# Hybrid attention and PEER layer on one core: gather steps moved between the attention heads and the query stage

## The chip, the cores and the metric

One Trainium2 chip, one of its cores. The metric is the device time of one execution of the program, in microseconds (us). Engines are called as in the profile: PE (TensorE matmuls) and PEld (its weight loads), DVE (VectorE), ACT (ScalarE), POOL (GpSimd), SP (SyncE, here only a DMA queue).

## The reference, cut to what matters

One decoder layer over 512 tokens of 1024 values. First a mixer: 8 heads of dilated window attention (head group A), 8 heads of stick-breaking attention (head group B), one output projection, a layer norm. Then PEER: each token picks 128 of 16384 single-neuron experts and takes a gated sum over them; a second layer norm.

```
mix = hybrid_mixer(x, w_in[layer], w_out[layer])
x = layer_norm(DEEPNORM_ALPHA * x + mix, ...)
...
q = (x @ w_query).reshape(b, s_len, PEER_HEADS, 2, PEER_KEY_DIM // 2)
scores = einsum('bshpc,hpnc->bshpn', q, sub_keys)      # 8 heads x 2 halves x 128 keys
top_s, top_i = lax.top_k(scores, PEER_TOPK)            # 16 of each half
...
best_s, best_pos = lax.top_k(cand_s, PEER_TOPK)        # 16 of the 256 sums
gates = jax.nn.softmax(best_s, axis=-1)
...
u = jnp.take(expert_u, ib, axis=0)
h = jnp.einsum('td,ted->te', xb, u)
act = gb * jax.nn.gelu(h, approximate=False)
vv = jnp.take(expert_v, ib, axis=0)
y = jnp.einsum('te,ted->td', act, vv)
```

## The kernel before

The 512 tokens are four blocks of 128. The PEER sum is done in two ways. For blocks 0 and 1 the kernel **gathers**: for each of the 128 chosen experts of a token, one indirect DMA from the POOL queue brings one row of `peer_u` (later of `peer_v`) per token, 128 rows of 4 KB, 512 KB in all. For blocks 2 and 3 it computes all 16384 experts **densely** on PE: `h` products with streamed `uT` tiles (L849), Gelu, a product with a scattered gate table, and `y` products with streamed `peer_v` tiles (L1106).

There are 512 gathers, numbered in order: 0 to 127 are `peer_u` for block 0, 128 to 255 `peer_v` for block 0, then the same for block 1. `gather(n)` (L732) issues one. `gather_use(n)` consumes one on DVE: a `peer_u` gather is one multiply-and-sum (L741), a `peer_v` gather one multiply-and-add (L752; the second one is a plain scaling, L749). After gather 127 the 128 sums go through Gelu on ACT (L743), DVE scales `x` (L744), and before gather 128 DVE multiplies the sums by the gates (L747), which waits for that Gelu. The generator `gathers` uses one gather per step and keeps eight further ones issued (nine buffers), up to `limit`, which is 256 until block 1 is routed. `take(n)` takes n such steps. 64 gathers are used before the part of the program that the change touches.

That part is written out by hand (`tc.manual_schedule()`): each engine runs its instructions in the order in which the loops emit them.

- **The heads** (loop over i from -1 to 33). 32 tasks: eight heads of group A for block 3 and eight of group B for block 1 mixed (tasks 0 to 15), then eight of group B for block 2 (16 to 23) and for block 3 (24 to 31). A task is a generator of six steps spread over four iterations. For group B (`head_b`): scores on PE (L341, L343), three activations (L347 to L349), one DVE operation (L351, emitted in iteration i = its task number), cumulative sums on PE (L353, L355, one iteration later), an exponential (L357), the product with the values on PE (L361). Each iteration ends with some gather steps.
- **The fills**. From i = 16 on the output projection of block 1, from i = 28 on that of block 2 is filled in, two steps per iteration (`next(fill, None)`): `project_out` has four steps of two products (L499) for each half c, then `add_out` on DVE (L459 and its half statistics, L145); then `normalize` in three steps: statistics with two tiny activations (L160, L161) and L514 on DVE; L163 to L166 and L519 on DVE; transposes on PE (L172) with copies by ACT (L525). `epilogue` copies and transposes a finished head group (L372, L172, L396).
- **Behind the loop**: the last epilogue (block 3) with gather steps between, what is left of the fill, `project_out(3)` with a gather step after each of its steps, and `normalize(3)` with two gather steps.
- **The query stage** (loop over it from 0 to 17): PE computes a query projection (`q_mm`, L597, L599) and scores (`q_scores`, L610, copied by ACT at L612); two iterations later DVE finds the best 16 of each row for three blocks, in five rounds of three operations (`topk_ops`, L536 to L544), with a gather step after each of the first QGATH rounds. `run_ahead` puts in pieces of the dense `h` products.
- **Behind it**: `route_steps(2)` on DVE, then 64 steps that build the gate table while `route_steps(3)` and `route_steps(1)` run, then the dense stage, in which all gathers that are left are spread evenly (`pre` is the count used so far).

Of the kernel before, what the change touches and what calls it, by code (L numbers as in the profile page):

```python
# [74 lines left out]
KT = 6  # L75
MIXB = (5, 4, 2)
PRE0 = 64
QGATH = 4
QH = 2
PRE1 = 7  # L80
GSTEP = 24
# [11 lines left out]
def build(ctx, nc, tc, a):  # L93
# [45 lines left out]
    def bank(nm):  # L139
        if nm == "mm":  # L140
            nm = next(mm_banks)
        return (ps_h if nm == "h" else ps_f).tile([P, 512], F32, name=nm, bufs=2 if nm == "h" else 1)
# [161 lines left out]
    def group(tb):  # L304
        st = {"po": bank("h")}
        for n_ in ("nm", "z", "rz"):
            st[n_] = work.tile([P, NH], F32, name=n_, bufs=3)
        return st
# [80 lines left out]
    def xcol(tb, ks):  # L389
        return x1[:, ks] if tb == 1 else xf[:, ks, (tb - 2) * P:(tb - 1) * P]  # L390
# [10 lines left out]
    def epilogue(kind, tb, st):  # L401
        o = (close_a if kind == "a" else close_b)(st)
        yield
        place([(o, tb, 0 if kind == "a" else 4)])
        yield
# [22 lines left out]
    def chain(*steps):  # L428
        for s_ in steps:
            yield from s_  # L430
# [17 lines left out]
    def head(steps, n):  # L448
        for _ in range(n):
            if next(steps, steps) is steps:  # L450
                return
            yield
# [4 lines left out]
    def add_out(tb, c, ps):  # L457
        sl = slice(c * 512, (c + 1) * 512)
        nc.vector.scalar_tensor_tensor(x2[:, tb, sl], x2[:, tb, sl], ALPHA, ps, op0=OP.mult, op1=OP.add)  # L459
        if c == 0:  # L460
            sts[tb] = stats_tile()
        half_stats(x2[:, tb], sts[tb], c)
# [30 lines left out]
    def project_out(tb):  # L493
        for c in range(2):
            ps = bank(("m2", "tr")[c])
            for kq in range(4):
                for k in range(2):
                    kk = 2 * kq + k
                    nc.tensor.matmul(ps, xcol(tb, kk), wo[c, kq][:, k], start=kk == 0, stop=kk == KD - 1)  # L499
                yield  # L500
            add_out(tb, c, ps)

    def normalize(tb):
        t = [] if tb == 0 else ln1
        if tb == 0:
            for n in ("ln1_g", "ln1_b"):
                t.append(wst.tile([P, D], F32, name="w", bufs=WBUF))
                nc.sync.dma_start(t[-1], a[n].to_broadcast([P, D]))
        r = x2[:, tb]
        s_ = stats_steps(sts[tb])  # L510
        mv = next(s_)
        halves = [slice(g * 512, (g + 1) * 512) for g in range(2)]
        for sl in halves:
            nc.vector.scalar_tensor_tensor(r[:, sl], r[:, sl], mv[:, 0:1], t[0][:, sl], op0=OP.subtract, op1=OP.mult)  # L514
        if tb:
            yield
        mv, rs = next(s_)
        for sl in halves:
            nc.vector.scalar_tensor_tensor(r[:, sl], r[:, sl], rs, t[1][:, sl], op0=OP.mult, op1=OP.add)  # L519
        yield  # L520
        for g in range(2):
            tr = transpose4(r[:, g * 512:(g + 1) * 512], "a" if g and tb == 0 else "tr")
            ks = slice(4 * g, 4 * g + 4)
            if tb:
                nc.scalar.activation(xcol(tb, ks), tr, AF.Copy)  # L525
            else:
                nc.scalar.activation(x0(ks), tr, AF.Copy)
        yield
# [396 lines left out]
    with tc.manual_schedule():  # L925
        def take(n):
            for _ in head(gs, n):
                pass
# [8 lines left out]
        for i in range(-1, NTASK + 2):  # L937
            def go(j):
                if 0 <= j < NTASK:
                    next(live[j])  # L940

            next(lo_, None)
            new = i + 1 < NTASK
            if new:
                kind, tb, h = tasks[i + 1]
                if h == 0:
                    sts_[kind, tb] = group(tb)
                live[i + 1] = (head_a if kind == "a" else head_b)(tb, h, sts_[kind, tb], ("a", "b", "m0", "m1")[(i + 1) % 4])
                go(i + 1)
            go(i)  # L950
            for g_ in list(after):
                if next(g_, g_) is g_:
                    after.remove(g_)
            if new:
                go(i + 1)
            next(fill, None)
            go(i - 1)
            go(i - 1)
            take(2 if i >= 14 else i % 4 > 0)
            next(fill, None)  # L960
            if i >= 2:
                go(i - 2)
                kind, tb, h = tasks[i - 2]
                if h == NH - 1:
                    after.append(epilogue(kind, tb, sts_[kind, tb]))
            if (fill_at := {16: 1, 28: 2}.get(i)):
                fill = chain(fill, project_out(fill_at), normalize(fill_at))
        for g_ in after:
            for _ in g_:
                take(1)  # L970
        for _ in fill:
            pass
        qs.close()
# [6 lines left out]
        for _ in project_out(3):  # L980
            take(1)
# [9 lines left out]
        for it in range(18):  # L991
# [7 lines left out]
            if it >= 2:  # L999
                ops = [topk_ops(tb, it - 2, scs[it - 2][:, t]) for t, tb in enumerate(PARTS[1])]  # L1000
                for r in range(5):
                    for o_ in ops:
                        next(o_)
                    if r < QGATH:
                        take(1)
# [232 lines left out]
```

## Time and profile before

| what | us |
|---|---|
| median of 3 runs | 1536.68 |
| the 3 runs | 1536.68, 1538.01, 1508.45 |
| the profiled execution, its own time | 1511.87 |
| its span, first to last instruction | 1510.1 |

Over the span PE is busy for 92%, DVE 80%, POOL 45%, ACT 34%. The page's 40 slices of 37.8 us show three stretches: up to slice 21 the DMA rate swings between 163 and 393 GB/s; in slices 22 to 37 it stands at 406 to 410 GB/s; the last three slices are the end of the dense stage and the final norms. The granted PE clock is 0.96 over the whole. "Busy" of PE is modelled, so the reader looks for the engine whose instructions follow each other without a gap and whom others wait for, stretch by stretch.

### The profile page before, as it was taken

The page shows a single profiled execution, that of the slowest core. Times are in us where ns is not written, and L with a number is a line of the kernel's source. Part 1 is how long each engine was busy: PE and PEld are TensorE (multiplying, and loading weights), DVE is VectorE, ACT ScalarE, POOL GpSimd, SP SyncE. Part 2 cuts the span into 40 slices and gives each one's busy share as a digit, 9 for nine tenths or more (in the row PEclk, how much of TensorE's full clock was granted, in tenths as well). Part 3 has the DMA queues.
Part 4 walks back from the last instruction along what each step waited for, and adds up shares of the span by engine and source line. Part 5 has one row for each costly group of instructions (what it writes and reads, how often), then busy time and mean ns, then how long its engine had stood idle before and what let it go on. Part 6 is the DMA issues. An engine that isn't in the chain of part 4 may idle for free.

```text
span 1510.1 us, 19683 instructions
## 1 busy us (share of the span) xinstructions
PE 1382.3 (92%) x6686; PEld 1120.0 (74%) x6686; DVE 1203.2 (80%) x2481; ACT 507.0 (34%) x1059; POOL 682.2 (45%) x526
## 2 busy tenths in 40 slices
PE   7989888999989998288889999999999999999796
PEld 3658676776659987277678888888888888878575
DVE  0128988886669999999998877778778878788887
ACT  1422333453412111199952222222223222222342
POOL 0000476754555444302556555555556556566200
PEclk9889999999999999599999999999999999999898
DMA  8756799896689999568999999999999999999872
GB/s 287 232 172 229 281 336 330 294 393 209 206 302 331 367 312 363 163 220 268 288 329 410 410 408 410 410 409 409 409 410 410 409 410 410 410 409 406 334 247 93
DMA packets 163220, 495.94 MB, mean 328 GB/s; under 512 B 15376, under 2 KB 48288, under 8 KB 163120
## 3 DMA queue, kind: packets, MB, share of 16 engines
q0 software_dynamic: 74304, 270.13, 47.6%
q1 hardware_dynamic: 86432, 218.66, 39.6%
q10 hardware_dynamic: 2384, 5.90, 1.0%
q8 instruction: 53, 0.87, 0.2%
q14 instruction: 47, 0.39, 0.1%
HBM read 477.78 MB, written 16.84 MB: 328 GB/s over the span
## 4 chain that ended last, share of the span: by engine, by line
DMA 36%; PE 27%; DVE 23%; issue 8%; ACT 4%; POOL 2%; SPq 0%; ACTq 0%; POOLq 0%; DVEq 0%
DMA g<-peer_u,eidx 17%; DMA g<-peer_v,eidx 14%; PE y L1106 5%; PE h L849 4%; DVE yg L752 4%; DVE x L752 3%; POOL g L732 2%; DMA v<-peer_v 2%; ACT o L815 2%; PE m L261 2%; PE m L499 1%; DVE o L806 1%; PE tr L499 1%; DVE vl L123 1%; DVE g L741 1%
## 5 line engine op out<-in xcount | busy, mean ns | idle before, releaser
L732 POOL DMA_INDIRECT g<-peer_u,eidx x256 | 343.2, 1341 | 388.8 <-DVE topi L544 145.7
L732 POOL DMA_INDIRECT g<-peer_v,eidx x256 | 333.1, 1301 | 338.0 <-DVE x L752 101.3
L849 PE MATMUL h<-xf,w 128*128 128x256 f32 x2048 | 475.4, 381 | 7.4 <-ACT gl L841 7.4
L849 PEld LDWEIGHTS h<-xf,w 128*128 128x128 f32 x2048 | 385.0, 191 | 60.3 <-ACT gl L841 7.8
L741 DVE SCALAR_TENSOR_TENSOR g<-g,x 128x1024 f32<-128x1024 f32 x256 | 307.7, 1222 | 71.0 <-DMA g<-peer_u,eidx 69.6
L1106 PE MATMUL y<-vh,a 128*128 128x512 f32 x928 | 289.6, 417 | 14.2 <-ACT a L1092 10.1
L1106 PEld LDWEIGHTS y<-vh,a 128*128 128x128 f32 x928 | 176.3, 191 | 56.6 <-ACT a L1092 13.0
L752 DVE SCALAR_TENSOR_TENSOR x<-g,hg,x 128x1024 f32<-128x1024 f32 x128 | 163.8, 1279 | 28.6 <-DMA g<-peer_v,eidx 27.3
L752 DVE SCALAR_TENSOR_TENSOR yg<-g,hg,yg 128x1024 f32<-128x1024 f32 x126 | 161.4, 1281 | 18.1 <-DMA g<-peer_v,eidx 16.4
L123 DVE TENSOR_TENSOR vl<-v,vh 128x1024 fp32r<-128x1024 f32 x122 | 148.8, 1220 | 23.1 <-ACT vh L1061 21.9
L1106 PE MATMUL y<-vl,a 128*128 128x512 f32 x464 | 147.5, 400 | 0.7 <-DVE vl L123 0.7
L1061 ACT ACTIVATE vh<-v 128x1024 fp32r<-128x1024 f32 x122 | 128.6, 1054 | 40.8 <-DMA v<-peer_v 22.0
L1092 ACT ACTIVATE a<-gl 128x512 fp32r<-128x512 f32 x58 | 36.5, 629 | 268.5 <-DVE gl L1086 233.9
L841 ACT ACTIVATE gl<-h 128x256 f32<-128x256 f32 x128 | 48.3, 378 | 222.9 <-PE h L849 213.0
L1106 PEld LDWEIGHTS y<-vl,a 128*128 128x128 f32 x464 | 87.8, 190 | 22.0 <-DVE vl L123 2.0
L815 ACT ACTIVATE o<-o1b,sg 128x128 f32<-128x128 bf16 x256 | 83.4, 400 | 2.7 <-DVE o1b L800 2.4
L261 PE MATMUL m<-w,x0f 128*128 128x256 f32 (+1 forms) x128 | 48.5, 520 | 9.1 <-DMA x0f<-xT 7.9
L821 PEld LDWEIGHTS m<-o,o 128*128 128x128 f32 x304 | 39.0, 195 | 21.1 <-ACT o L815 14.4
L821 PE MATMUL m<-o,o 128*128 128x128 f32 x304 | 42.9, 285 | 12.1 <-ACT o L815 5.6
L127 PE MATMUL m<-wl,x2h 128*128 128x512 f32 x96 | 41.1, 428 | 9.8 <-DVE wl L123 9.7
L806 DVE TENSOR_TENSOR o<-sg,c_small 128x512 f32<-128x512 f32 x64 | 43.8, 685 | 0.7 <-PE a L821 0.6
L261 PEld LDWEIGHTS m<-w,x0f 128*128 128x128 f32 x128 | 24.0, 200 | 26.6 <-issue 11.1
(261 smaller groups left out, 1859.5 us busy)
## 6 DMA issues: line engine op xcount, KB each, us to landing
w<-uT SPq DMA_DIRECT2D x128, 512.0 KB
v<-peer_v SPq DMA_DIRECT2D x128, 512.0 KB
w<-w_in SPq DMA_DIRECT2D x47, 512.0 KB
gt<-gd SPq DMA_DIRECT2D x15, 960.0 KB
w<-peer_wq SPq DMA_DIRECT2D x16, 512.0 KB
wq<-peer_wq SPq DMA_DIRECT2D x16, 512.0 KB
gd<-stage SPq DMA_DIRECT2D x15, 512.0 KB
gd<-stage SPq DMA_DIRECT2D x15, 448.0 KB
```

Source lines behind the costliest of these rows:

```text
L123: nc.vector.tensor_sub(parts[1], src, parts[0].bitcast(F32))
L261: nc.tensor.matmul(ps[:, ch * wd:(ch + 1) * wd], x0f[:, kk], w[:, k], start=kk == 0, stop=kk == KD - 1)
L732: nc.gpsimd.indirect_dma_start(out=u, out_offset=None, in_=a["peer_v" if kind else "peer_u"], in_offset=bass.IndirectOffsetOnAxis(ap=eidx[ ...
L741: nc.vector.scalar_tensor_tensor(u, u, 1.0, x, op0=OP.mult, op1=OP.mult, accum_out=hs[:, j:j + 1])
L752: nc.vector.scalar_tensor_tensor(acc, u, hs[:, j:j + 1], acc, op0=OP.mult, op1=OP.add)
L806: nc.vector.tensor_tensor(hot2[s], gate[tb][1][:, 0, t:t + TG, None].to_broadcast([P, TG, P]), iota[:, None, :].to_broadcast([P, TG, P]), ...
L815: nc.scalar.activation(hot[s][:, j], o1b[:, :, j], AF.Copy, scale=gate[tb][1][:, 1, t + j:t + j + 1])
L821: nc.tensor.matmul(gps[s][:, j * P:(j + 1) * P], o2[:, j], o1[:, j], start=True, stop=True)
L841: nc.scalar.activation(gls[c // 2][:, c % 2], ps[:, :ND], AF.Gelu)
L849: nc.tensor.matmul(hps[c][:, :ND], us[c][:, k], xf[:, k], start=k == 0, stop=k == KD - 1)
L1061: nc.scalar.activation(vsp[c][0], vs[c], AF.Copy)
L1106: nc.tensor.matmul(yps[t][hf], s_, w_[:, hf * 512:(hf + 1) * 512], start=c == 0 and n == 0, stop=c == P - 1 and n == len(terms) - 1)
```

## The change

Three counts and one extra step change; no instruction is new.

- `QGATH` goes from 4 to 3: three gather steps for each query iteration from it = 2 on instead of four.
- In the loop over the heads the iterations from i = 24 on take three gather steps instead of two.
- The last epilogue takes two gather steps after each of its two steps instead of one.
- `project_out` gets one more `yield` between the products of half 0 and its `add_out`. In a fill, the `add_out` of half 0 and all that follows come half an iteration later; in `project_out(3)` it is one more gather step.

```diff
-QGATH = 4
+QGATH = 3
...
                     nc.tensor.matmul(ps, xcol(tb, kk), wo[c, kq][:, k], start=kk == 0, stop=kk == KD - 1)
                 yield
+            if c == 0:
+                yield
             add_out(tb, c, ps)
...
             go(i - 1)
             go(i - 1)
-            take(2 if i >= 14 else i % 4 > 0)
+            take(3 if i >= 24 else 2 if i >= 14 else i % 4 > 0)
             next(fill, None)
...
         for g_ in after:
             for _ in g_:
-                take(1)
+                take(2)
```

## Rows read from the trace of the kernel before

**Rows 1.** Stages: length, busy us per engine (instructions), granted PE clock, DMA share, GB/s
```profile
371.60:425.70 54.10, 54.10 (x274) 37.95 (x272) 29.77 (x51) 22.59 (x37) 26.16 (x21) 0.99 0.65 213
...
425.70:449.50 23.80, 18.42 (x48) 8.95 (x48) 18.72 (x36) 2.68 (x6) 14.94 (x10) 0.86 0.87 330
...
465.80:598.40 132.60, 125.18 (x723) 113.85 (x722) 132.60 (x449) 18.29 (x41) 63.78 (x66) 0.97 0.95 345
...
598.40:640.50 42.10, 12.99 (x53) 10.67 (x52) 40.92 (x136) 5.73 (x13) 13.93 (x12) 0.64 0.57 191
...
640.50:775.00 134.50, 116.72 (x740) 98.42 (x739) 131.56 (x353) 123.55 (x354) 44.13 (x23) 0.99 0.82 263
...
775.00:1430.00 655.00, 640.12 (x2838) 538.13 (x2837) 534.10 (x687) 171.18 (x263) 371.83 (x277) 0.99 1.02 406
```

**Rows 2.** Timeline, query stage, DVE: start, length, instruction [idle before]
```profile
465.83 0.67 DVE L536 MAX8 top<-sc 128x8 f32<-128x128 f32 x3
...
590.70 1.28 DVE L752 SCALAR_TENSOR_TENSOR yg<-g,hg,yg 128x1024 f32<-128x1024 f32 x1
...
591.89 0.10 DVE L538 MATCH_VALUE_LOAD topi<-top,sc 128x8 f32 x1
...
598.41 0.42 DVE L1017 CAST iob<-c_small 128x512 bf16<-128x512 f32 x1
```

**Rows 3.** Timeline, query stage, PE
```profile
550.81 0.83 PE L610 MATMUL m<-skT,qT 128*128 128x128 f32 x6
...
557.58 0.83 PE L610 MATMUL m<-skT,qT 128*128 128x128 f32 x6
...
559.12 0.83 PE L610 MATMUL m<-skT,qT 128*128 128x128 f32 x6
```

**Rows 4.** Timeline behind the heads, PE and DVE
```profile
424.21 0.69 DVE L459 SCALAR_TENSOR_TENSOR x<-x,tr 128x512 f32<-128x512 f32 x1 [6.98 <-PE tr L499]
...
427.30 1.22 DVE L741 SCALAR_TENSOR_TENSOR g<-g,x 128x1024 f32<-128x1024 f32 x1
...
429.59 0.15 DVE L163 TENSOR_TENSOR lw<-lw 128x1 f32<-128x1 f32 x1
...
431.25 1.09 PE L172 MATMUL tr<-c_ident,x 128*128 128x128 f32 x4 [3.52 <-DVE x L519]
...
433.93 8.70 PE L499 MATMUL m<-wo,xf 128*128 128x512 f32 x16
...
442.47 7.03 PE L499 MATMUL tr<-wo,xf 128*128 128x512 f32 x16
```

**Rows 5.** Timeline around gather 127's Gelu, ACT and DVE
```profile
460.81 1.28 ACT L743 ACT_TABLE_LOAD   x1
...
462.10 0.31 ACT L743 ACTIVATE hg<-hg 128x128 f32<-128x128 f32 x1
...
462.45 0.29 DVE L747 TENSOR_TENSOR hg<-hg,gate 128x128 f32<-128x128 f32 x1 [3.48 <-ACT hg L743]
...
463.62 0.49 ACT L612 ACTIVATE sc<-m 128x384 f32<-128x384 f32 x1 [0.18 <-PE m L610]
```

**Rows 6.** Timeline, the first fill's norm, PE
```profile
362.19 0.78 PE L361 MATMUL h<-v,su 128*128 128x64 f32 x6
...
363.76 0.23 PE L343 MATMUL m<-maskb,identb 128*128 128x128 bf16 x1
...
366.35 1.12 PE L172 MATMUL tr<-c_ident,x 128*128 128x128 f32 x4 [2.36 <-DVE x L519]
...
371.62 1.17 PE L361 MATMUL h<-v,su 128*128 128x64 f32 x6
```

**Rows 7.** Timeline, head tasks 27 and 28, DVE and PE
```profile
386.63 0.69 DVE L351 SCALAR_TENSOR_TENSOR su<-m,su 128x512 f32<-128x512 f32 x1 [1.10 <-ACT su L349]
...
393.37 1.08 PE L353 MATMUL m<-su,c_tri 128*128 128x512 f32 x2
```

**Rows 8.** Chain of waits, dense stage: start, length, what
```profile
1049.46 20.30 DMA g<-peer_u,eidx
```

## The prediction

> **What bounds the kernel now.** I read the slices of the page first, then the busy times by stage, then the timeline of the stages that the change touches, and the waits there. The slices part the run at about 790 us: behind it the DMA rate is flat, ahead of it it is not. The stage rows [rows 1] say who sets the pace. Over the heads of block 3 (371.6 to 425.7 us) PE is busy for all of 54.10 us and DVE for 29.77: PE sets it, DVE has 24 us free. In the query stage (465.8 to 598.4) DVE is busy for all of 132.60 us. In the routing and the gate table (598.4 to 775) DVE has 40.92 of 42.10 and 131.56 of 134.50. From 775 to 1430 the DMA share is 1.02 at 406 GB/s. So ahead of 775 us the engines decide, and what they save up to there starts the dense stage earlier by as much; behind it bytes decide, and each gather not used by then is paid at the DMA rate.
>
> **Gather steps counted.** Before: 64 early, 51 in the loop over the heads (11 up to i = 13, two in each of the 20 iterations behind), 2 in the last epilogue, 8 in `project_out(3)`, 2 in its norm: 127 when the query stage begins; then 2 + 2 + 16 x 4: 195 at its end. After: 64 + 61 + 4 + 9 + 2 = 140, and 4 + 16 x 3 more: 192. So 16 steps leave the query stage, 13 go to the heads and the stretch behind them, 3 are left to the dense stage.
>
> **Query stage: -19.0 us.** DVE begins the first round at 465.83 and the routing's first operation at 598.41 [rows 2]: 132.6 us for 16 iterations, 8.29 each. A `peer_v` step costs from its start at 590.70 to the next instruction at 591.89, 1.19 us [rows 2] (less than the 1.28 shown, since ends overlap). 16 x 1.19 = 19.0; an iteration comes to 7.10. PE needs from 550.81 to 557.58, 6.77 us, for the same iteration [rows 3], and had put out its last scores at 559.12, 39 us ahead of DVE [rows 2, 3]. So DVE still sets the pace, but by 0.33 us per iteration only.
>
> **The extra half step in the first fill: -3.0 us (0 to -4.5).** Block 1's norm stops PE: behind its instruction at 363.76 it waits until 366.35 for L519 (2.36 us), and comes back slow [rows 6]. The product that took 0.78 at 362.19 takes 1.17 at 371.62 [rows 6], so the 6.4 us between 366.35 and the end of that one hold some 2.1 us lost. With the extra `yield`, L163 to L519 are emitted ahead of the gather steps of iteration 22 instead of behind those of iteration 21, and the transposes behind the cumulative sums of task 21 instead of ahead of them. PE has work in the wait. 2.36 + 2.1 = 4.5 at most; nothing if DVE's order leaves the wait as it is. I take 3, nearer to the most, since PE's work between is there.
>
> **The third step in iterations 24 to 33: 0 us.** A `peer_u` step costs half of 427.30 to 429.59, 1.145 us [rows 4]; ten more are 11.5 us in 24 us of DVE's free time [rows 1]. A step of the heads asks 0.69 [rows 7] + 3 x 1.145 = 4.1 us of DVE; PE takes 54.1/10 = 5.4 per iteration [rows 1], less for the first few. DVE falls back there by a microsecond or two, but task 27's L351 starts at 386.63 and PE reads it at 393.37 [rows 7]: six microseconds in hand. If that cover were gone, the ten steps would cost their 11.5. In transfers the stage had 213 GB/s; ten gathers of 0.524 MB in 54.1 us add 97: 310, against 406 in the dense stage [rows 1].
>
> **Behind the heads: +2.5 us (to +7.9).** Here the change costs. The chain is: L459 of half 1 at 424.21, statistics and L514, two gather steps from 427.30, L163 at 429.59, transposes on PE at 431.25, `project_out(3)` from 433.93 [rows 4]. Three things alter.
> First, in PE's order the value product of task 30 now stands ahead of half 1's last products: +1.0 by [rows 6] (six products 0.78, eight about 1.0).
> Second, four gather steps stand between L514 and L163, not two, and by the count above they are 125 to 128. So Gelu's wait falls in here: three steps (3.44), then ACT's Gelu and DVE's multiply and step 128. From Gelu's start at 462.10 to L747 at 462.45 is 0.35 [rows 5]; with 0.2 before it, 0.29 for L747 and 1.19 for the step I count 5.5 in place of 2.3, +3.2. PE, its transposes, and all of `project_out(3)` are queued behind L163. The table load of 1.28 [rows 5] runs while DVE is still in steps 125 to 127; without that cover it is 1.28 more.
> Third, this wait leaves the query stage, where DVE stood 3.48 us for Gelu [rows 5]. The first scores were copied by 464.11 [rows 5] and DVE came 1.7 later [rows 2]; now it finds them ready: -1.7.
> Sum 1.0 + 3.2 - 1.7 = 2.5. PE's pause grows by about 4 us, and behind the present one (granted clock 0.86 over this stage [rows 1]) half 0 takes 8.70 us against 7.03 for half 1 [rows 4]; were all of half 0 at the lower clock level, it would be 14.06: +5.4, the upper end. The ninth step in `project_out(3)` lies in DVE's wait for these products.
>
> **Three gathers later: +3.9 us (0 to 3.9).** 3 x 0.524 MB at 406 GB/s [rows 1]. Nothing, if PE and not DMA spaces the dense stage: PE is busy for 640 of its 655 us [rows 1]. I take the DMA's price, as its share is the full one.
> A page of the Trainium skill speaks of this rate: HBM Reference, Specifications, gives about 358 GB/s as a core's share with both cores of a memory domain streaming, and about 425 for a core alone. By the share the three would cost 4.4 (estimate), the sum would be half a microsecond worse. The stage here moves 406, nearer to the figure for a core alone.
>
> **Sum.** -19.0 - 3.0 + 0 + 2.5 + 3.9 = -15.6 us. Against the profiled execution's 1511.87 that gives 1496.3. That execution lies 24.8 below the median shown; the three runs lie at 1508.45 and at 1536.68 and 1538.01, 28 apart for one and the same program, more than this change moves. Set against the median, the sum gives 1521.1, my number; the range must hold both places. The sum's own bounds: -19.0 - 4.5 + 2.5 + 0 = -21 and -19.0 + 0 + 7.9 + 3.9 = -7.2.
>
> **Rivals.**
> *The gap behind the heads eats half* (0.20). The PE clock stays low over half 0 and the first fill gains nothing: -7.2, 1529.5. For it: PE's clock falls at each pause of this size in the trace [rows 4, 6]. Against: half of the lower rate is already in the 8.70.
> *PE spaces the dense stage* (0.10). Then the three gathers are free: -19.5, 1517.2. For it 640 of 655, against it a DMA share of 1.02 [rows 1].
> *Nothing is left* (0.09). What DVE saves is lost ahead of 775 us, by PE's pace in the query stage: its margin is 0.33 us per iteration, and 16 iterations longer by 1.0 for a late weight tile would take the 15.6. 1536.7. Against: PE ran its 16 iterations without such a wait while the DMA carried 345 GB/s [rows 1, 3], and fewer gathers ask for less.
> *Slower: gathers land too late* (0.06). With eight ahead, a landing of T gives a gather each T/8. In the dense stage one took 20.30 us [rows 8], 2.54 each: three would take 7.6 us where an iteration of the heads lasts 5.4 and one of the query stage 7.1. Ten times 2.2, and 16 times 0.5: +30, in sum +14: 1551. It begins to cost at 3T/8 = 5.4, a landing of 14.4 us. Against: four gathers per 8.29 us came without a gap in DVE's 132.60 [rows 1, 2], so they landed within 16.6 us, at a higher rate (345 GB/s) than the 310 asked of the heads.
> The forecast itself has 0.55.
>
> **Range and chances.** Its lower end is the lowest run less 21: 1487; its upper end is the highest run less 5, 1533, which takes in the forecast, PE-spaced and half-eaten cases wherever the runs fall. 2% of the median, about what a measurement of this kernel can tell from no change, is 31 us; no case of gain reaches it alone. Faster by over 2% takes runs that fall at the lower place more often than before: 0.13. Slower by over 2% takes late landings at their worst together with the higher place: 0.04. Within 2%: 0.83.
>
> **What would show it.** In the changed profile: query iterations of 7.1 us on DVE with no idle, and their whole stretch near 113.5; L519 of block 1's norm followed by transposes without a two-microsecond stop of PE; no wait of L351's readers in the heads; L743 between the last epilogue and `normalize(3)`, L163 some 5.5 us behind L514, `project_out(3)` about a microsecond later than before (-3 + 4.2); the DMA plateau starting some 19 us earlier. It is wrong if DVE waits for gathers or scores before 600 us, or if the plateau starts earlier and the end does not.

## The result and the profile after

| | us |
|---|---|
| before, median of 9 runs beside those of after | 1510.87 (1508.45 to 1543.34) |
| after, median of 9 runs | 1518.97 (1493.44 to 1526.99) |
| ratio after : before, executions of one kind | 0.9916, 95% interval 0.9889 to 0.9942 |

Executions of either kernel come in two lengths some 28 us apart (a stretch at half PE clock from 300 us on, called the early half clock below, makes the longer one), the medians mix them, and the ratio compares only the shorter ones. So the change takes off 0.84%: 12.7 us of 1510.87, between 8.8 and 16.8. The sum of the prediction, -15.6, lies inside that interval. The profiled execution of after has the early half clock, so it is read stage by stage. Its line numbers behind L500 are two higher than those of before (L741 is L743).

The page of after, its span and the granted PE clock in 40 slices of 38 us, in tenths:

```profile
span 1522.9 us, 19706 instructions
...
PEclk9889999957998999799999999999999999999898
```

The 5 and the 7 in the ninth and tenth slice are the half clock: 300 to 364 us, ahead of most of what the change touches. Stages of after, the columns as in [rows 1]: a window in the low clock; block 3's heads; the stretch to L459; the query stage; the routing; the dense stage:

```profile
350.00:360.00 10.00, 10.00 (x47) 9.32 (x46) 7.57 (x15) 4.72 (x10) 5.50 (x4) 0.50 0.50 157
371.60:425.70 54.10, 52.55 (x282) 38.12 (x281) 44.58 (x81) 29.21 (x52) 34.10 (x23) 1.00 0.63 204
425.70:450.30 24.60, 24.60 (x101) 15.02 (x101) 18.19 (x32) 4.34 (x7) 20.03 (x16) 1.00 0.91 318
495.60:609.00 113.40, 113.40 (x677) 104.08 (x676) 113.40 (x432) 18.62 (x39) 44.95 (x48) 1.00 0.92 319
609.00:651.00 42.00, 23.03 (x102) 19.63 (x101) 41.26 (x137) 7.19 (x17) 13.27 (x11) 0.80 0.65 221
794.00:1430.00 636.00, 623.19 (x2776) 524.81 (x2776) 516.32 (x666) 163.81 (x255) 378.15 (x271) 0.99 1.03 409
```

DVE's 44.58 us in the heads stand against 29.77 in [rows 1]: the third step. The query stage lasts 113.40 us against 132.60, and DVE is busy for all of it. The dense stage moves 409 GB/s against 406.

Where the time went, between marks that both kernels have (the start of an instruction each, in order: first L499 of the first fill, L351 of tasks 24 and 31, the first MAX8 of the query stage, the routing's cast, the first gate-table operation, the last `y` product). The third column sets after against another execution of before with the same early half clock (h2_before_again, below); the fourth sets a second profile of after without it (e1_all) against the profile of before.

| stretch | forecast | after, both with the early half clock | after, both without it |
|---|---|---|---|
| first fill up to task 24 | -3.0 | -5.0 | -3.8 |
| task 24 to task 31 | 0 | +1.5 | **+6.9** |
| task 31 to the first MAX8 | +2.5 | +3.0 | +3.3 |
| query stage | -19.0 | -19.0 | -19.1 |
| routing | 0 | -0.2 | 0.0 |
| gate table and dense stage | +3.9 | +5.1 | +4.8 |
| sum | -15.6 | -14.6 | -7.9 |

Five of six lines are near their terms. One is not: task 24 to 31 in the fourth column, 6.9 us, about half of the gain. That column belongs to one execution of 1501.37 us, the second longest of the six of e1_all (1492.38 to 1504.27): its stages sum to -7.9, where the ratio of all six (0.9913) makes -13.1. So not every execution need lose as much there. And ahead of the first fill, where no edit but the last below reaches, the eleven profiles without the early half clock differ by 12 us (first L499 at 325.7 to 338.1), so single executions are compared by stage and not by their time.

**The query stage**, timeline of DVE and of PE (start, length, instruction):

```profile
495.57 0.68 DVE L538 MAX8 top<-sc 128x8 f32<-128x128 f32 x3 [3.68 <-ACT sc L614]
...
524.53 1.26 DVE L754 SCALAR_TENSOR_TENSOR x<-g,hg,x 128x1024 f32<-128x1024 f32 x1
525.71 0.08 DVE L540 MATCH_VALUE_LOAD topi<-top,sc 128x8 f32 x1
...
609.04 0.40 DVE L1019 CAST iob<-c_small 128x512 bf16<-128x512 f32 x1
```

```profile
580.70 0.83 PE L612 MATMUL m<-skT,qT 128*128 128x128 f32 x6
...
587.47 0.83 PE L612 MATMUL m<-skT,qT 128*128 128x128 f32 x6
...
589.00 0.83 PE L612 MATMUL m<-skT,qT 128*128 128x128 f32 x6
```

As [rows 2, 3] with one step less: 113.47 us in 16 iterations, 7.09 each; a step still takes 1.18; PE still needs 6.77 and ends 20 us ahead of DVE instead of 39.

**Behind the heads**, DVE, then PE, then ACT:

```profile
450.33 0.69 DVE L459 SCALAR_TENSOR_TENSOR x<-x,tr 128x512 f32<-128x512 f32 x1 [0.77 <-PE tr L499]
...
453.42 1.22 DVE L743 SCALAR_TENSOR_TENSOR g<-g,x 128x1024 f32<-128x1024 f32 x1
...
457.58 0.28 DVE L749 TENSOR_TENSOR hg<-hg,gate 128x128 f32<-128x128 f32 x1
...
459.10 0.15 DVE L163 TENSOR_TENSOR lw<-lw 128x1 f32<-128x1 f32 x1
...
479.42 0.69 DVE L459 SCALAR_TENSOR_TENSOR x<-x,tr 128x512 f32<-128x512 f32 x1 [0.68 <-PE tr L499]
...
482.51 1.28 DVE L754 SCALAR_TENSOR_TENSOR x<-g,hg,x 128x1024 f32<-128x1024 f32 x1
483.70 0.15 DVE L163 TENSOR_TENSOR lw<-lw 128x1 f32<-128x1 f32 x1
```

```profile
460.76 1.09 PE L172 MATMUL tr<-c_ident,x 128*128 128x128 f32 x4 [6.92 <-DVE x L521]
...
463.45 9.07 PE L499 MATMUL m<-wo,xf 128*128 128x512 f32 x16
472.35 7.03 PE L499 MATMUL tr<-wo,xf 128*128 128x512 f32 x16
```

```profile
454.50 1.28 ACT L745 ACT_TABLE_LOAD   x1
456.97 0.31 ACT L745 ACTIVATE hg<-hg 128x128 f32<-128x128 f32 x1 [1.19 <-DVE g L743]
...
481.30 0.20 ACT L160 ACTIVATE lw<-lw 128x1 f32<-128x1 f32 x1 [15.72 <-DVE mv L157]
481.52 1.28 ACT L161 ACT_TABLE_LOAD   x1
482.82 0.20 ACT L161 ACTIVATE lw<-lw 128x1 f32<-128x1 f32 x1
```

L459 to L163 takes 8.77 us against 5.38 in [rows 4]; three steps, Gelu, the gates' product and step 128 stand between, and Gelu's table load (454.50) is hidden behind steps 125 to 127, as was said. PE's pause is 6.92 us against 3.52, and half 0 behind it 9.07 against 8.70. New is the load at 481.52: it stands between L160 and L161 of `normalize(3)`, which in before ran back to back (451.42 and 451.65). It costs nothing: L161 is done at 483.02, while DVE is in a gather step until 483.70, and L163 starts there. That is 4.28 us behind L459 (479.42), against 4.23 in before (449.54 and 453.77), where no load stood.

**The heads**, DVE and POOL:

```profile
413.45 0.69 DVE L351 SCALAR_TENSOR_TENSOR su<-m,su 128x512 f32<-128x512 f32 x1
...
417.48 0.69 DVE L351 SCALAR_TENSOR_TENSOR su<-a,su 128x512 f32<-128x512 f32 x1
...
437.72 1.23 DVE L743 SCALAR_TENSOR_TENSOR g<-g,x 128x1024 f32<-128x1024 f32 x1 [1.44 <-DMA g<-peer_u,eidx]
```

```profile
412.35 1.98 POOL L734 DMA_INDIRECT g<-peer_u,eidx  x1 [0.30 <-issue]
414.64 1.44 POOL L734 DMA_INDIRECT g<-peer_u,eidx  x1 [0.30 <-issue]
```

Iterations follow each other on DVE by 4.03 us, near the 4.1 worked out. PE waits nowhere for L351. But POOL issues one gather in 1.74 to 2.29 us (the instruction and 0.30 behind it), some 6.0 for three, and DVE uses three in 4.03. From 422 to 438 us DVE waits seven times for a gather, 0.2 to 1.4 us each, 5.6 in all. Its last step ends at 449.56, 0.8 ahead of PE's products for L459. The work still fits, and there is hardly any room left.

### The profile page after: what moved, and what is told of

Its sections match the earlier page's. It is cut to its first block, busy times and chain, and to the rows that moved or that the text cites. A ratio compares the mean times of both kernels' runs of the same rounds, so it can differ in the third digit from the quotient of the medians.

```text
span 1522.9 us, 19706 instructions
## 1 busy us (share of the span) xinstructions
PE 1410.8 (93%) x6686; PEld 1141.9 (75%) x6686; DVE 1202.9 (79%) x2481; ACT 511.4 (34%) x1062; POOL 697.2 (46%) x526
## 4 chain that ended last, share of the span: by engine, by line
PE 35%; DMA 31%; DVE 21%; issue 7%; ACT 4%; POOL 2%; another core or an unknown queue 0%; SPq 0%; ACTq 0%; POOLq 0%; DVEq 0%
DMA g<-peer_v,eidx 14%; DMA g<-peer_u,eidx 12%; PE y L1108 8%; PE h L851 8%; DVE x L754 3%; DVE yg L754 3%; DMA v<-peer_v 2%; POOL g L734 2%; ACT o L817 2%; PE m L499 2%; PE m L261 2%; DVE o L808 1%; PE tr L499 1%; PE h L333 1%; PE h L361 1%
## 5 line engine op out<-in xcount | busy, mean ns | idle before, releaser
L734 POOL DMA_INDIRECT g<-peer_u,eidx x256 | 353.0, 1379 | 385.0 <-DVE topi L546 145.2
L734 POOL DMA_INDIRECT g<-peer_v,eidx x256 | 338.3, 1322 | 340.8 <-DVE yg L754 94.7
L743 DVE SCALAR_TENSOR_TENSOR g<-g,x 128x1024 f32<-128x1024 f32 x256 | 306.5, 1222 | 60.5 <-DMA g<-peer_u,eidx 59.0
L261 PEld LDWEIGHTS m<-w,x0f 128*128 128x128 f32 x128 | 24.7, 205 | 25.7 <-issue 11.9
```

What stands on the lines that cost most here:

```text
L261: nc.tensor.matmul(ps[:, ch * wd:(ch + 1) * wd], x0f[:, kk], w[:, k], start=kk == 0, stop=kk == KD - 1)
L734: nc.gpsimd.indirect_dma_start(out=u, out_offset=None, in_=a["peer_v" if kind else "peer_u"], in_offset=bass.IndirectOffsetOnAxis(ap=eidx[ ...
L743: nc.vector.scalar_tensor_tensor(u, u, 1.0, x, op0=OP.mult, op1=OP.mult, accum_out=hs[:, j:j + 1])
```

## The experiments

Theory: the terms of the sum are right, and what the fourth column loses is PE's clock behind block 1's norm, where the fill now stands differently. Rivals: the third step in the heads takes it (by POOL's pace), or Gelu's new place does.

**The whole change again.** There is no edit against after.

> The whole change once more, for a second execution to read by stages. The theory of the sum (DVE sets the query stage, PE hides the third step in the heads, each gather left over is paid at the DMA rate in the dense stage): about 13 to 16 us shorter than before, query stage from its first MAX8 to the routing's first cast 113.5 us in place of 132.6, dense stage 3 to 4 us longer. The rival that descriptor generation on POOL, and not PE, sets the end of the heads: DVE's last gather steps of the heads lie behind the last output projection product of block 2, and the heads end several us later than before. A further suspicion from the profile after: the norm of block 3 shows a second activation table load of 1.28 us between its two tiny activations, 1.3 us on the way to the query stage; it should be there again.

Measured: 1495.3 us median, ratio 0.9913 (0.9879 to 0.9947), so the first result holds. Its stages stand in the table above. PE at the norm of the first fill, then PE's clock from 360 us on (columns as in [rows 1]):

```profile
362.54 0.66 PE L172 MATMUL tr<-c_ident,x 128*128 128x128 f32 x4 [0.88 <-DVE x L521]
363.89 0.66 PE L172 MATMUL tr<-c_ident,x 128*128 128x128 f32 x4 [0.69 <-ACT x L527]
...
365.26 2.07 PE L341 MATMUL a<-qB,kB 64*128 64x128 f32 x8
...
383.61 1.16 PE L341 MATMUL m<-qB,kB 64*128 64x128 f32 x8
```

```profile
360.00:365.00 5.00, 3.44 (x23) 2.61 (x21) 4.86 (x11) 3.02 (x6) 0.44 (x1) 0.98 0.02 3
365.00:370.00 5.00, 5.00 (x17) 3.87 (x17) 3.56 (x8) 2.12 (x4) 4.08 (x4) 0.50 0.47 128
370.00:375.00 5.00, 5.00 (x20) 4.05 (x19) 3.76 (x7) 1.77 (x4) 2.99 (x4) 0.50 0.86 320
375.00:380.00 5.00, 5.00 (x21) 4.40 (x20) 4.12 (x7) 1.44 (x3) 1.62 (x2) 0.50 0.83 285
380.00:385.00 5.00, 5.00 (x24) 3.37 (x23) 3.23 (x6) 2.90 (x6) 3.65 (x4) 0.81 0.64 197
```

The wait for the norm has shrunk from 2.36 us [rows 6] to 0.88, and the 0.69 for ACT's copy behind it is left, as in before. Then PE, busy without a gap, stands at half clock (1.2 GHz instead of 2.4) for more than 15 us: eight products take 2.07 us instead of 1.16. In before the windows of 5 us behind its longer wait show a shorter stretch:

```profile
365.00:370.00 5.00, 2.96 (x10) 2.26 (x11) 4.89 (x11) 1.88 (x4) 2.96 (x3) 0.56 0.62 175
370.00:375.00 5.00, 5.00 (x24) 4.01 (x24) 2.47 (x5) 1.39 (x3) 3.69 (x4) 0.76 0.72 219
375.00:380.00 5.00, 5.00 (x37) 4.43 (x36) 3.65 (x7) 3.75 (x7) 1.68 (x1) 1.00 0.68 238
```

**One part each.** First `QGATH` alone:

```diff
-QGATH = 4
+QGATH = 3
```

> Only the third step per query iteration: nothing is taken earlier, so 16 gathers are left to the dense stage. Theory of the sum: the query stage is 19.0 us shorter, the dense stage 16 x 1.29 = 20.6 us longer, in all +1.6 us, no difference to be measured. Rival, that the gain of the change is the shorter query stage itself and the dense stage has room for gathers (PE spaces it): about -15 to -19 us.

Measured: 1.0023 (1.0002 to 1.0044), some +3.5 us. The query stage is 113.44 us, 19.1 less; gate table and dense stage together are 21.0 longer than the mean of three profiles with before's count of gathers (862.9 us, see below), 1.31 per gather for 16 gathers. Taking steps out of the query stage is worth nothing by itself; the gain comes from where they go.

The extra `yield` alone:

```diff
+            if c == 0:
+                yield
```

> Only the extra yield ahead of the first add_out (and the one gather step more that it brings in the last output projection). Theory of the sum: 3.0 us less in the norm of block 1 (PE's stop of 2.4 us gone), 1.0 us more behind the heads, one gather fewer in the dense stage (-1.3), in all -3.3 us. Rival, that PE stops there as long as before because DVE's order leaves the wait: 0 to -1.3 us.

Measured: 0.9969 (0.9948 to 0.999), -4.7 us, near the -3.3 expected. Its profile (1509.19 us, the second longest of nine at 1501.33 to 1510.7) shows less: up to task 24's L351 it gains 3.9 us, from there to task 31 it loses 3.9 again (35.39 us against 31.53; granted clock 0.74 from 366 to 386 us), and its stages sum to -1.0. The heads have before's gather steps here and Gelu its old place, and the low clock is there all the same: neither the third step nor Gelu brings it on.

The `yield` and the gathers moved to the heads, with `QGATH` left at 4:

```diff
+            if c == 0:
+                yield
...
-            take(2 if i >= 14 else i % 4 > 0)
+            take(3 if i >= 24 else 2 if i >= 14 else i % 4 > 0)
...
-                take(1)
+                take(2)
```

> The extra yield, the third step in iterations 24 to 33 and two steps in the last epilogue, but four steps per query iteration as before. 13 gathers are used earlier and none later. Theory of the sum: -3.0 in the first fill, +2.5 to +4 behind the heads, 13 x 1.29 = 16.8 us less in the dense stage: -16 to -17 us, as good as the whole change or a microsecond or two better, since a step costs 1.19 us in the query stage and 1.29 in the dense stage. Rival, that the query stage's fourth step is what cost the time: between 0 and -4 us.

Measured: 0.9944 (0.9921 to 0.9966), -8.5 us: a miss. Gate table and dense stage give back 11.9 us for 13 gathers (851.0 against 862.9), where 16.8 were expected, and task 24 to 31 takes 38.44 us, 6.9 more than in before, at a clock of 0.57 from 366 to 386. Its stages sum to -7.5, so here the profile and the time agree. Nearly the same stretch stands in e1_all (38.40 us). It is 3.0 us longer than in e3, which has no third step in the heads; whether the third step lengthens the stretch, no run tells.

**The wait taken away.** The norm's transposes one half step later still, the second one into a free bank:

```diff
         yield
+        if tb:
+            yield
         for g in range(2):
-            tr = transpose4(r[:, g * 512:(g + 1) * 512], "a" if g and tb == 0 else "tr")
+            tr = transpose4(r[:, g * 512:(g + 1) * 512], ("m2" if tb else "a") if g else "tr")
```

> The whole change, and in addition the transposes of the norms of blocks 1 to 3 half an iteration later still, the second one into another PSUM bank, so that PE waits neither for L521 nor for the first copy in the first fill. Theory that the two short waits of PE there (0.9 and 0.7 us) bring on the half clock that made the heads behind them 4 to 7 us longer than before: the clock stays at its full level, the stretch from task 24's to task 31's L351 falls from 38.4 us to 30 to 33, and the whole is 5 to 7 us faster than the whole change. Rival, that the clock falls there for another reason (what PE does in those iterations, not that it waits): stretch at 38 us again, the whole at most 1 us faster.

Measured: 0.9886 (0.9841 to 0.993), -17.2 us. Its profile has the early half clock. In the eight profiles of that kind with the extra `yield` the clock stands at 1.00 behind the norm, with the later transposes or without, so this one doesn't show the cause. The same edit without any gather step moved in the heads (before, with the extra `yield` and this) was run twice:

> The kernel before with the extra yield and the later transposes, no other step moved: the part on the norms alone, without any third gather step. Theory of PE's waits: the low clock behind block 1's norm is gone here too, so 9.8 + 31.5 us from the transposes to task 31's L351 become 5 + 30 to 31 and the whole is 8 to 9 us faster than before (4 to 6 more than the extra yield alone). Rival, that the clock falls for the third steps' sake: as the extra yield alone, 3 to 5 us faster than before.

> The later transposes alone, without the waits: 4.7 us from the transposes to task 24's L351 and 29 to 31 from there to task 31's, by both theories; a spell of half clock here would speak against the waits.

As times these were inconclusive (1494.46 and 1501.89 us without the early half clock, then 1503.0 and 1505.85). As profiles they answer. PE at the norm in h4_late_only:

```profile
358.20 0.61 PE L172 MATMUL tr<-c_ident,x 128*128 128x128 f32 x4
358.65 0.60 PE L172 MATMUL m<-c_ident,x 128*128 128x128 f32 x4
...
361.09 1.16 PE L341 MATMUL b<-qB,kB 64*128 64x128 f32 x8
```

PE doesn't wait, the clock stays at 1.00, and task 24 to 31 takes 29.86 us in both runs, the shortest of all; e3_halfstep_only is the same kernel without the later transposes. Over all profiles without the early half clock: the six whose PE waits at this norm (before, e1_all, e2, e3, e4, j2 below) show a low clock behind it, the five whose PE doesn't (g3, g4, h4, i4, j1) show 1.00.

**Gelu out of the way.** After, with no steps in the last epilogue, two in each of the first four steps of `project_out(3)` instead, and one table set that has both of the norm's functions loaded right behind block 0's Gelu; then this and the later transposes together:

```diff
                 nc.scalar.activation(hs, hs, AF.Gelu)
+                if tb == 0:
+                    nc.scalar.preload_act_table_set("natural_log_exp_and_others")
...
-                take(2)
+                pass
...
-        for _ in project_out(3):
-            take(1)
+        for n_, _ in enumerate(project_out(3)):
+            take(2 if n_ < 4 else 1)
```

> The whole change, but the last epilogue's four gather steps are taken in the first four steps of the last output projection (two each), so that Gelu and its wait lie beside that projection's products; and the activation tables for Ln and Exp are loaded by one instruction behind Gelu. Theory of the sum: L163 of block 2's norm comes 3.1 us behind the add_out in place of 8.8 (5.7 us earlier), the table load of 1.3 us between the two tiny activations of block 3's norm is gone, and DVE takes the four steps where it waited for PE anyway: 6 to 7 us faster than the whole change. Rival, that DVE's gather steps then hold up add_out in the last projection: the gain behind the heads is given back there, 0 to 2 us.

> Both: later transposes and Gelu beside the last projection. If the two causes are apart, the gains add: 11 to 14 us faster than the whole change, some 25 us faster than before. If the low clock comes for another reason, 6 to 8.

Measured: 0.9885 (0.9853 to 0.9917) and 0.9855 (0.9829 to 0.9881), that is -17.4 and -21.9 us. DVE behind the heads in g3_both:

```profile
415.86 0.69 DVE L459 SCALAR_TENSOR_TENSOR x<-x,tr 128x512 f32<-128x512 f32 x1 [3.36 <-PE tr L499]
...
418.94 0.15 DVE L163 TENSOR_TENSOR lw<-lw 128x1 f32<-128x1 f32 x1
```

L459 to L163 is 3.08 us against 8.77. So the cost behind the heads was the order of the steps, and it could be had back. The two gains add up: 4.5 and 4.7 us beyond after singly, 9.2 together. With the one table set loaded ahead, no load stands at L160 or L161 any more (442.01 and 442.24).

**More steps to the heads.** g3_both with three steps from i = 17 on, run twice:

```diff
-            take(3 if i >= 24 else 2 if i >= 14 else i % 4 > 0)
+            take(3 if i >= 17 else 2 if i >= 14 else i % 4 > 0)
```

> As both, and the third gather step already from iteration 17 on: seven gathers more in the heads, seven fewer in the dense stage. Theory of the sum: 7 x 1.1 = 7.7 us faster than both, if DVE and POOL have room in the first fill (POOL is busy for half the time there). Rival, that POOL's descriptor generation (1.4 to 2.0 us a gather while DVE works through gather steps, 3 per iteration of 4 us) makes DVE late in iterations 24 to 27: the last L351 comes later than in both and the gain is 0 to 3 us. Gelu falls into the heads in this one and may cost a microsecond there.

> The version with both changes behind the heads and in the norm and the third gather step from iteration 17 on, timed in more rounds: its profile summed to 29 to 30 us less than before (1480.4 against 1510.1 of span); expected 1.8 to 2.1% faster than before.

Measured: 0.9836 (0.9778 to 0.9894) in the second run, -24.8 us; the shortest execution of the first is 1482.18. Seven more gathers leave the dense stage, which with the gate table takes 858.7 us against 868.1 with after's count. The heads pay part of it: from the first L499 to L459 they take 87.7 us against 84.6 in both g3_both and h4_late_only.

**Repeated for the profile.** These were to give further profiles of after, of before and of g2, above all without the early half clock:

> The whole change, another profile, to see whether the half clock in the heads behind block 1's norm comes in every execution. Theory (PE's two short waits at the transposes bring it on): the stretch from task 24's to task 31's L351 is again well over 33 us, near the 38.4 us of the last profile. Rival (chance of one execution): near 32 us.

> The kernel before, another profile, for the same reason: its first profile had 31.5 us from task 24's to task 31's L351 and 9.8 us from the transposes to task 24's; PE waits 2.4 us at the transposes here. If that wait brings on the low clock for as long as it did in the first profile, 9 to 11 us and 31 to 33 us again.

> The whole change, a further profile. If PE's two short waits at the transposes of block 1's norm bring on the half clock: 34 to 39 us from task 24's to task 31's L351. If the last profiles' spell was chance: 31 to 33 us.

> As the run before it: 34 to 39 us by the waits, 31 to 33 if by chance.

> The version that moves Gelu beside the last projection and keeps the waits at the transposes: 34 to 39 us from task 24's to task 31's L351 by the waits, 31 to 33 if by chance. Behind the heads: add_out to L163 in 3.1 us again.

All five profiles have the early half clock. In the four with the extra `yield` none follows at block 1's norm, though PE waits 0.87 us there (i1 and i2: 31.52 us from task 24 to 31); in h2, behind before's wait of 2.36 us, 6.8 us at half clock follow all the same. h2 gave the third column of the table, i2 the ratio 0.9933 (0.9882 to 0.9985), i3 0.9874 (0.9835 to 0.9912), and i3's L459 to L163 is 3.09 us again.

**The early half clock itself.** At the start of the heads PE waits 1.33 us for an activation (L324 for L320), in before as in after. PE there in after:

```profile
299.06 0.66 PE L324 MATMUL a<-c_ident,su 128*128 128x128 f32 x4 [1.33 <-ACT su L320]
...
300.37 1.06 PE L324 MATMUL b<-c_ident,su 128*128 128x128 f32 x4
```

In the profile of before the same second row takes 0.61. So two products whose result nobody reads were put into that wait, in before and in g4:

```diff
+            if i == 1:
+                warm = bank("m2")
+                for _ in range(2):
+                    nc.tensor.matmul(warm, ident, v[:, 0, :512], start=True, stop=True)
             go(i - 1)
```

> The version with the third step from iteration 17 on, the later transposes and Gelu beside the last projection, and in addition two products of 128x512 into an unused PSUM bank ahead of the first transposes of the heads, where PE waits 1.33 us for the exponential of task 0 (the result is not read). If that wait brings on the half clock of 60 us: all executions lie between 1478 and 1490 us. If not: executions near 1510 us are among them as often as before.

> The kernel before, and only those two products where PE waits 1.33 us at the beginning of the heads. If that wait brings on the half clock: all executions lie between 1501 and 1516 us and none near 1540. If not: 1540 as often as before, about four in ten.

PE in j2_before_filled, then the window from 310 to 320 us of it, and of after:

```profile
296.94 1.94 PE L960 MATMUL m<-v,c_ident 128*128 128x512 f32 x4
298.71 0.60 PE L324 MATMUL a<-c_ident,su 128*128 128x128 f32 x4
```

```profile
310.00:320.00 10.00, 10.00 (x70) 8.27 (x69) 7.46 (x17) 6.89 (x19) 5.51 (x5) 1.00 1.03 408
```

```profile
310.00:320.00 10.00, 10.00 (x36) 7.65 (x35) 5.58 (x11) 3.82 (x10) 2.09 (x2) 0.50 1.03 410
```

Measured: before with the filler 1.0018 (0.9998 to 1.0039), but all its 12 runs lie at 1500.52 to 1515.13 us, where 3 of the 17 of before beside them lie at 1538 to 1540. By itself that is weak: at 3 in 17, none of 12 would come up by chance one time in ten. g4 with the filler: all 6 runs at 1475.88 to 1482.16, where 6 of the 11 of g4 and h3 without it lie at 1507.86 to 1515.56; none of 6 would be chance one time in a hundred. Its median is 1479.05, the ratio 0.9809 (0.9791 to 0.9827): -28.8 us of 1510.39. It is the version that beats both kernels.

## Why the prediction was wrong, and where it was right

Two steps failed: the term of the extra half step, whose account left out PE's clock behind the wait that remains, and the last step, from the sum to the number and its chances. The other terms held, or were off by little over a microsecond.

**Counting the query stage** was right: 16 steps of 1.19 make -19.0, measured -19.0 and -19.1; PE's margin of 0.33 us per iteration was enough, so "nothing is left" fell.

**Three gathers later** (+3.9): gate table and dense stage together take 883.9 us with 179 gathers used at the end of the query stage (e2), 868.1 with 192 (nine executions, 866.8 to 869.8), 862.9 with 195 (before, h2, j2: 861.8 to 865.0), 863.7 with 196 (e3, h4, i4, which have the ninth step in `project_out(3)`), 858.7 with 199 (three) and 851.0 with 208 (e4). From 192 to 195 that is 5.2 us, 1.3 over the term and over its upper end, with a scatter of 3 us for one count; over the whole row a gather is worth 1.13 us (32.9 for 29) against the forecast's 1.29. "PE spaces the dense stage" (nothing for the three) fell.
The share of 358 GB/s in the Trainium skill, HBM Reference, Specifications, would make it 4.4 us (estimate); that scatter doesn't tell it from the term, and the rate of the stage, 409, is not the share.

**Behind the heads** (+2.5): +3.0 and +3.3. L459 to L163 grew by 3.4 for +3.2 forecast, the PE order cost 0.9 for +1.0 (e3: 17.46 against 16.57, where nothing else differs), the first MAX8 came 1.7 sooner behind the last projection in e1_all (14.64 us from the end of its products, against 16.33), as said. In after it came only 0.1 sooner: ACT's copy of the first scores started 1.6 us behind their product, and what held it the trace does not name. Half 0 took 0.4 longer. What was not seen is the table load between L160 and L161, and it does no harm: in before Gelu came behind `normalize(3)`, now it comes ahead, and the two functions of the norm bring a load each, but the gather step behind L516 covers the second. Half 0 went from 8.70 to 9.07, far from the 14.06 of the bound, so "the gap eats half" did not come in this place.

**The third step** (0): holds at L459, while PE's clock is full. Task 24 to L459 takes 47.33 us in g3_both with three steps and 47.32 in h4_late_only with two. The reason was half: DVE's time was costed, POOL's was not, and POOL's pace (6.0 us for three) is what uses up the cover; with seven steps more (g4) 3.1 us show. Of "gathers land too late" the mechanism is there, DVE's waits of 0.2 to 1.4 us, and the price isn't, since PE had the reserve. The prediction took a wait of DVE for gathers or scores ahead of 600 us as a sign of being wrong. In after both came. The seven waits cost nothing at L459: it comes 48.99 us behind task 24's L351, 0.9 over the 48.10 of before, and that is the PE order's. The other is 3.68 us for the first scores (495.57), the wait that the first MAX8 had there.

**The extra half step** (-3.0): this is the term that failed. The wait shrank as said, and up to task 24 the gain is -3.8. But the prediction took "2.36 + 2.1" as all there was, the wait and the slow products behind it, and ended its account at the product after the norm. It did not ask what PE's clock does behind the wait that is left. In all three profiles with that wait and without the early half clock it falls to half, and tasks 24 to 31 take 3.9 us (e3) or 6.9 (e1, e4) more: the term's -3.0 came out as 0.0 and +3.1. By time the loss is less plain: e4 came out at -8.5 where -16 to -17 were expected, 4.9 of it for the gathers, and e3 at -4.7 where -3.3 was expected, as if the term held. The first profile of before has 6.8 us at half clock at this place, and [rows 6] has the fall itself: a bound of its own for the clock, with the sign of a loss, was due there. The rival "the gap eats half" gave -7.2, near the -7.9 of e1's stages, by luck: it put the loss at half 0.

**The number and the chances** were the larger error. The sum was set against 1536.68, a median of three runs of which two had the early half clock, and gave 1521.1. That lies 10.2 us above the 1510.87 of before's nine runs: a gain had become a time longer than that of before. After's median, 1518.97, came near it by luck, because five of its nine runs had the early half clock as well. The last step then took 2% (31 us) as about what a measurement of this kernel can tell, and gave 0.83 to a difference within it. It does lie within 2%, but it is not nothing: like against like, executions lie within about half a percent of their middle, and the comparison told 0.84% from nothing, with an interval of plus and minus 0.3%. A sum of -15.6 with bounds of -21 and -7.2 was, by its own terms, a forecast of a gain.

**What stays open.** That PE's wait at the norm goes with the low clock behind it is shown by its removal (five profiles against six), though the edit takes the wait away by moving the transposes, and no run moves them and keeps the wait. The wait alone does not decide it: in the six profiles that have the wait of 0.87 us and the early half clock (after: 395.40), none follows. Nor does its length set the length of the stretch: behind before's 2.36 us it lasts 3.4 us (j2), 6.8 (before, h2) and 10.2 (e2), behind the shorter wait 10.2 (e3) and 17.1 (e1, e4). What sets it, and how many executions of after have it, no run tells.

## What to carry to other kernels

Cost a moved step twice, in the stage that it leaves and in the one that it goes to, and there on every engine that serves it: DVE had 24 us free here, while POOL, which issues the gathers, had next to none. When a wait of PE is shortened, take away the rest as well, or count the slow products behind it: in two of three profiles 6.9 us, half of this change's gain, lay in what followed a wait of 0.9 us. And add a sum to the time of the execution that it was read from, not to a median that mixes executions with and without a stretch of 28 us.

## What the runs showed of the hardware

- A wait of 1.33 us can be followed by some 60 us at half PE clock with PE busy for 10.00 of every 10 us (after: 0.50 from 300 to 364 us), in some executions of a program and not in others: some 28 us. With two products in the wait (1.94 us of PE) none of the 18 runs of two kernels had it.
- Two activations can each bring a table load though one set has both functions: in after 464.30 for L160 and 481.52 for L161, in g3_both, with that one set loaded ahead, none. The Trainium skill, ScalarE: Activation LUTs, What ACT_TABLE_LOAD costs, gives about 1.28 us for the load and a further 1.38 for a drain. The load agrees with the trace (1.28); the drain is not in these rows, L161 starts at 482.82, 0.02 us behind the load's end.
- The POOL instruction of a gather takes 0.94 us in the query stage, where DVE's steps lie between short operations, and 1.44 to 1.99 where DVE runs multiply-and-sums of 128x1024 back to back (after, 404 to 425 us). The Trainium skill, GPSIMD Engine Reference, Specifications, says that GpSimd shares its SBUF interfaces with VectorE, with contention where a VectorE operation has two SBUF inputs, among others; that fits, and no run here separates it from other causes.
